# Gated trunk layer on one core: panel order p, v, va, ob, the samples' mLSTM beside va, the output gate in the third branch, eight merge-gate panels by seven products

## The chip, the cores and the metric

The kernel runs on one core of a Trainium2 chip. The metric is the device time of one execution in microseconds (us). Three runs of the kernel before gave 1856.19, 1856.73 and 1857.31 us; the median is 1856.73.

The engines have these names in the profile: PE is TensorE (matmuls; PEld its weight loads), DVE is VectorE, ACT is ScalarE, POOL is GpSimd, SP is SyncE, which here only issues transfers. "L308" is line 308 of the kernel. PEq, SPq, ACTq are the queues (sequencers) of an engine.

## The reference

One layer of a trunk, for a prompt of 1024 tokens and eight samples of 8 tokens (64 tokens with their own recurrent state), width 1024, all in float32:

```
h    = rmsnorm(x) * (1 + scale) + shift          # shift, scale, gate from silu(c) @ w_mod
mg, u, va, za, q, k, v, ob, zb, ig, fg, p, zc = split(h @ w_in)
ya   = gelu(u) * sgu(layernorm(gelu(va))) * silu(za)    # sgu: 128x128 causal mixing of positions
yb   = head_layernorm(sigmoid(ob) * mlstm(q, k, v, ig, fg)) * silu(zb)
yc   = (windowed means of p - p) @ w_pool * scale * silu(zc)
merged = sigmoid(mg_a) * (ya @ w_a) + sigmoid(mg_b) * (yb @ w_b) + sigmoid(mg_c) * (yc @ w_c)
y    = rmsnorm(x + gate * (merged @ w_out))
```

The mLSTM has four heads, each with a 256x256 matrix state C. For the prompt C starts at zero and runs over eight chunks of 128 positions. For the samples each of the eight has its own C per head: 32 states of 256 KB that are read, multiplied by the samples' queries, updated by an outer product and written back. The outputs are y of both groups, the new states C, n and m, the last pooling rows, and the normalised va of the samples.

## The kernel before

**Precision and panels.** A float32 product is made of three products of a high and a low part (`split`, L206: a cast on ScalarE, the residual on VectorE): hi x hi, hi x lo, lo x hi. The weights come in panels of 256 columns, which a `Stream` loads through SP in quarters and splits in the order in which the panels were added (L419 to L433). Three routines run a panel:

- `seven` (L334) computes a panel by a scheme of seven block products in place of eight, with sums of weight blocks made on VectorE: 7 products x 4 blocks x 2 halves x 3 = 168 matmuls of 272 columns (L362).
- `b_panel` (L258) has features on the partitions: 6 units (two feature tiles, three token groups) x 8 x 3 = 144 matmuls of 362 or 364 columns (L270).
- `a_panel` (L296) has tokens on the partitions: eight units of 24 matmuls of 256 columns (L308), and a unit for the 64 sample tokens (L316).

**Order.** After the start (modulation, norm; to 177 us) come 25 panels by seven products: k, zb, zc, u, za and five of the twelve merge gate panels (`MG7`), to 708 us. Then `pool_branch` (L1183) runs p panels, each with a va panel behind it, four times (to 938 us). Then come four v panels and four ob panels, the remaining merge gate panels in `merge_gates` (L1280), the three branches a, b, c in the order c, a, b in `finish` (L1718; the third, b, from 1610 us) and the output projection (from 1750 us).

**Side work.** Everything that isn't a panel is written as generators that yield after each step. `side` is a list of them; a panel calls `tick(pace)` (L225), half of it in the middle of a unit and half at its end, and each whole tick that is owed advances the first generator of the list by one step. `pace` is 1.2 in `pool_branch`, `PACE` = 1.5 in the v and ob panels, and 1.4 from `merge_gates` on. So an a_panel owes 8.5 x pace ticks and a b_panel 6 x pace (none where it runs with `kouter`). Whatever is left is run out by `drain`. In `inputs_of_mixers` (L910), after the first v panel, the list becomes: `gen_gates` (the gates of the heads, with Exp and Ln), `gen_sgu` (nine tiles of three steps), `gen_gate` (the residual gate, 4 MB of w_mod, with the operand `scs`), `gen_sample` (the samples' mLSTM) and `gen_prompt` (the prompt's mLSTM, drained before the last panel of the second branch).

**Tiles.** Working tiles come from one pool of 34 equal buffers (`slot`, L182). An instruction that writes a new tile waits until a buffer is free, that is until the last reader of its former tile, a transfer included, is through. The activations h hold 17 of them (hhi 8, hlo 8, hstack) up to the end of the ob panels. `sgc` (w_sguT) and `bsgu` are loaded in `inputs_of_mixers` and given up at the end of `gen_sgu` (L1077); `scs` is given up at the end of `gen_gate` (L906).

**The sample loop** (L1675 on) runs 32 steps, head by head. A step x does on TensorE four matmuls of the split state Cs with the queries qz (L1682) and two of km with vst (L1687). Then `parts(x + 2)` makes Cs for the step after next (ScalarE's cast, L207, then VectorE's residual, L208). Then VectorE updates the state (L1692) and GpSimd issues its transfer out (L1694). After every second step, SP issues the load of the next but one pair of states (L1636), and GpSimd fills two columns (L1637, L1638). `head` (L1640) makes km and qz of the next head.

Of the kernel before, what the change touches and what calls it, by code (L numbers as in the profile page):

```python
# [8 lines left out]
F32 = mybir.dt.float32  # L9
# [7 lines left out]
TP = 1024  # L17
NB = 8
TS = 64
T = TP + TS  # L20
NH = 4
# [8 lines left out]
NQ = KT // QK  # L30
PW = 264
HT = 272
MG7 = 5
PACE = 1.5


class Stream:
# [121 lines left out]
class Builder:  # L159
# [254 lines left out]
    def body(self):  # L414
        i = self.i
        self.st = st = Stream(self)
        pan = {}
        for n in range(4):
            pan["q", n] = st.add(i["w_in"][self.PANEL["q"] + n])  # L419
        for nm_, n in self.SEVEN:  # L420
            pan[nm_, n] = st.add(i["w_in7"][self.PANEL7[nm_] + n], seven=True)
        for nm_, ns in [(x, (n,)) for n in range(4) for x in ("p", "va")] + [(x, range(4)) for x in ("v", "ob")]:
            for n in ns:
                g = nm_ == "v" and n == 0
                src = i["w_v0"] if g else i["w_in"][self.PANEL[nm_] + n]
                pan[nm_, n] = st.add(src, 264 if g else 256)
        for n in range(MG7, 12):
            pan["mg", n] = st.add(i["w_in"][self.PANEL["mg"] + n])
        for x in (2, 0, 1):
            for n in range(4):  # L430
                pan["br", x, n] = st.add(i["w_br"][x * 4 + n])
        for n in range(4):
            pan["out", n] = st.add(i["w_out"][n])  # L433
        self.pan = pan

        self.qd = self.dtile([8, 128, T], "qd")
        self.kd = self.dtile([8, 128, T], "kd")
        self.vd = self.dtile([T, D], "vd")
        self.od = self.dtile([T, D], "od")
        self.zd = [self.dtile([128, T], f"zd{f}") for f in range(8)]  # L440
        self.uzd = self.dtile([8, 128, T], "uzd")
        self.vad = self.dtile([T, D], "vad")
        self.zcd = [self.dtile([128, T], f"zcd{f}") for f in range(8)]
        self.b12d = self.dtile([4, 2, 128, 2 * HT], "b12d")
        self.yd = {0: self.dtile([8, 128, T], "yd0"), 2: [self.dtile([128, T], f"yd2_{f}") for f in range(8)]}
        self.ybd = self.dtile([8, 128, T], "ybd")
        self.mgd = [self.dtile([128, T], f"mgd{f}") for f in range(24)]
        self.rowd = self.dtile([2, NH, T], "rowd")
        self.decd = self.dtile([NH, 16], "decd")
        self.gated = self.dtile([9, D], "gated")  # L450

        tc = self.tc
        with tc.tile_pool(name="psumA", bufs=8, space=PSUM) as self.psum:
            self.start()
        with tc.tile_pool(name="pairs", bufs=1, space=PSUM) as self.pairs:
            self.seven_panels()
        with tc.tile_pool(name="psumB", bufs=8, space=PSUM) as self.psum:
            self.inputs_of_mixers()
            self.merge_gates()
            self.finish()  # L460
# [449 lines left out]
    def inputs_of_mixers(self):  # L910
        i, V, A, G, S = self.i, self.V, self.A, self.G, self.S
        self.w_sguT = self.slot([128, NH, 128], name="sgc")
        self.bsgu = self.slot([128, 8, 128], name="bsgu")
        S.dma_start(self.w_sguT, i["w_sguT"])
        self.w_sguS = self.cload("w_sguS")
        cm = self.slot([128, 128], name="keep")
        S.dma_start(cm, i["keep"])
        cms = self.slot([64, 64], name="keepS")
        S.dma_start(cms, i["keepS"])
        for j in range(2):  # L920
            S.dma_start(self.bsgu.rearrange("p (g j) t -> p g j t", j=2)[:, :, j, :], i["b_sgu"].partition_broadcast(128))
        self.maskp = self.cload("maskp")
        self.masks = self.cload("masks")
        self.bmask = self.cload("bmask")
        self.bif = self.cload("b_ifT")
        self.sm0 = self.cload("state_mT")
        self.n0 = self.cload("state_nT")
        self.ngc = self.cload("mnorm_gT")
        self.psc = self.cload("pool_scaleT")
        self.invc = self.const([128, NH, 16], "invc")  # L930
        S.dma_start(self.invc, i["invcnt"].partition_broadcast(128))
        for g in range(NH):
            V.tensor_tensor(out=self.w_sguT[:, g, :], in0=self.w_sguT[:, g, :], in1=cm, op=ALU.mult)
            V.tensor_tensor(out=self.w_sguS[:, g, :], in0=self.w_sguS[:, g, :], in1=cms, op=ALU.mult)
        V.tensor_scalar(self.bsgu, self.bsgu, 0.5, None, ALU.mult)
        V.tensor_scalar(self.ngc, self.ngc, 0.5, None, ALU.mult)
        V.tensor_scalar(self.psc, self.psc, 0.5, None, ALU.mult)

        self.drain()
        self.pool_branch()  # L940
        self.pace = PACE
        self.gsb = self.const([128, 9, 8], "gsb")
        for n in range(4):
            self.a_panel(self.pan["v", n], self.h, self.hs, self.evac_tok(n, self.vd, "copy"),
                         cols=264 if n == 0 else 256)
            if n == 0:
                self.side += [self.gen_gates(), self.gen_sgu(), self.gen_gate(), self.gen_sample(), self.gen_prompt()]
        for n in range(4):
            self.a_panel(self.pan["ob", n], self.h, self.hs, self.evac_tok(n, self.od, "tanh"))
        self.hs = None  # L950
# [231 lines left out]

    def pool_branch(self):  # L1183
        i, V, A, G, S = self.i, self.V, self.A, self.G, self.S
        self.pace = 1.2
        npp = self.const([128, 8, PB], "npp")
        nps = self.slot([128, 8, 8, PB], name="nps")
        for g in range(4):
# [85 lines left out]
                    G.dma_start(self.o["pool_s"], nps)  # L1274

            self.side.append(gen_pool())
            self.a_panel(self.pan["va", g], self.h, self.hs, self.evac_tok(g, self.vad, "gelu"))


    def merge_gates(self):  # L1280
        V, A, G, S = self.V, self.A, self.G, self.S
        self.pace = 1.4
        for n in range(MG7, 12):
            st = {}

            def evac(f, g, ps, n=n):
                g0, w = GROUPS[g]
                if g == 0:
                    st[f] = self.slot([128, T], name="mg")
                A.activation(st[f][:, g0 : g0 + w], ps, AF.Tanh, scale=0.5)  # L1290
                if g == 2:
                    G.dma_start(self.mgd[2 * n + f], st.pop(f))

            if n < 11:
                self.b_panel(self.pan["mg", n], self.h, evac)
            else:
                self.acts = {}
                for _ in self.prep_y(2):
                    pass
                while self.side and self.banks:  # L1300
                    self.advance(self.side)
                self.b_panel(self.pan["mg", n], self.h, evac, kouter=True, hook=self.prep_rest(2))
                self.h = None
# [256 lines left out]
    def gen_sample(self):  # L1560
        i, V, A, G, PE, S = self.i, self.V, self.A, self.G, self.PE, self.S
        m, c, t0 = TS, 8, TP
# [4 lines left out]
        v = self.slot([64, NH, 258], name="v")  # L1567
# [12 lines left out]
        p = self.ps()  # L1580
# [14 lines left out]
        for j in range(2):  # L1595
            p = self.ps()
# [14 lines left out]
        t1 = self.slot([64, NH, 258], name="t1")  # L1611
        for h in range(NH):
            p = self.ps()
# [4 lines left out]
            V.tensor_tensor(out=qv[:, :, d, :], in0=qv[:, :, d, :], in1=rb[:, 1], op=ALU.mult)  # L1618
        qh = self.slot([128, 2, 8, m], F32R, name="qh")
        self.split(qk[:, 0], qh[:, 0], qh[:, 1])  # L1620
        st6 = self.tmp.tile([128, NH, 6], F32, tag="st6", name=self.nm("st6"), bufs=2)
        den = self.tmp.tile([128, NH], F32, tag="den", name=self.nm("den"), bufs=2)
        no = self.const([128, NH, 8, 2], "no")
        qz = [self.slot([128, SW], F32R, name="qz") for _ in range(2)]
        for d in range(2):
# [49 lines left out]
        for x in range(32):  # L1675
# [22 lines left out]
            if bb == 7:  # L1698
                kms.pop(h)
                head(h + 1)  # L1700
                finish_head(h)
            yield
        o = self.slot([64, NH, 256], name="o")
        S.dma_start(o, self.od[t0:T].rearrange("t (h e) -> t h e", e=256))
        yield
# [4 lines left out]
        t1 = t2  # L1710
# [7 lines left out]
    def finish(self):  # L1718
# [6 lines left out]
        for xi, x in enumerate((2, 0, 1)):  # L1725
            for n in range(4):
# [34 lines left out]
                if n == 3 and xi == 1:  # L1761
                    self.drain()
                    self.side2.append(self.prep_y(1))
                if n < 3 or xi == 2:
                    self.b_panel(self.pan["br", x, n], acts, evac)
                else:
                    y = (2, 0, 1)[xi + 1]
                    while self.side2:
                        self.advance(self.side2)
                    while self.side and self.banks:  # L1770
                        self.advance(self.side)
                    self.b_panel(self.pan["br", x, n], acts, evac, kouter=True, hook=self.prep_rest(y))
                    self.prep_split(y)
                    self.acts[x] = None
        self.acts = None
        acts = [mh[k] for k in range(KT)]
        mstack = self.slot([128, KT, 128], F32R, name="mstack")
# [187 lines left out]
```

## Time and profile before

| | |
|---|---|
| median of three runs | 1856.73 us |
| profiled execution | 1857.86 us, its span 1856.1 us |
| mean granted clock of TensorE | 0.985 |
| ScalarE, GpSimd busy | 32%, 14% of the span |
| bytes moved | 270.42 MB, mean 146 GB/s |
| HBM read, written | 179.96 MB, 88.35 MB |

The span goes from the first instruction to the last; the difference of 1.8 us to the profiled execution's own time lies around it. A row of a group of instructions gives line, engine, operation, names of output and inputs, shapes, the number of instructions, then busy time and mean duration, and behind the second bar the idle time of the engine just before these instructions with what ended it. A row of a wait reads "who, line <- whom it waited for: us in all, times, longest". A row of a stretch gives its length, then busy time and instructions of each engine, TensorE's granted clock, the transfer engines' busy share and GB/s. Matmuls overlap in the pipeline, so the time between two starts, not the duration of one, is what a matmul costs in a full stage.

### The profile page before, as it was taken

To read this page: it belongs to the slowest core of one execution; us is meant where nothing else is said; L and a number is where in the kernel's file an instruction comes from. 1 tells how busy PE (TensorE), PEld (TensorE's weight loads), DVE (VectorE), ACT (ScalarE), POOL (GpSimd) and SP (SyncE) were. 2 spreads that over 40 slices of the span, in tenths; PEclk is the share of its full clock that TensorE was granted. 3 is DMA by queue.
4 is the path that set the end of the run, shared out by engine and by line. 5 is a ranking of instruction groups with operands and counts; after the bars stand their busy time and mean duration, and the time that the engine had idled before them with its cause. 6 is when DMAs were issued, how large, how long until landed. Compare 5 with 4: busy or idle time off the path is not lost.

```text
span 1856.1 us, 32242 instructions
## 1 busy us (share of the span) xinstructions
PE 1796.1 (97%) x13017; PEld 1777.4 (96%) x13017; DVE 1071.9 (58%) x2003; ACT 586.0 (32%) x1141; POOL 262.3 (14%) x427
## 2 busy tenths in 40 slices
PE   7888999999999999999999999999999999999998
PEld 7888999999999998999999899999999999999998
DVE  7777556665666542434527955664655766564444
ACT  5443333333333332222223125332333231131224
POOL 3440000000000001110011212321101101200023
PEclk8988999999999999999999999999999999999999
DMA  6332323332222334333335754776457577694422
GB/s 252 108 128 74 106 94 94 104 122 80 71 70 76 130 106 150 121 123 101 94 116 189 217 180 125 240 237 201 143 175 231 179 228 208 184 317 142 151 62 97
DMA packets 142152, 270.42 MB, mean 146 GB/s; under 512 B 19377, under 2 KB 66161, under 8 KB 142003
## 3 DMA queue, kind: packets, MB, share of 16 engines
q1 hardware_dynamic: 118786, 184.20, 31.4%
q0 software_dynamic: 23072, 83.91, 13.3%
q8 instruction: 102, 1.67, 0.4%
q14 instruction: 48, 0.39, 0.1%
q10 hardware_dynamic: 144, 0.26, 0.0%
HBM read 179.96 MB, written 88.35 MB: 145 GB/s over the span
## 4 chain that ended last, share of the span: by engine, by line
PE 86%; DVE 8%; issue 2%; DMA 2%; ACT 1%; POOL 1%; SPq 0%; POOLq 0%; DVEq 0%; ACTq 0%
PE ps L270 30%; PE ps L308 15%; PE p L362 8%; PE y L362 8%; PE z L362 8%; PE x L362 4%; PE ps L614 2%; PE ps L316 1%; PE ps L1466 1%; PE ps L1264 1%; PE ps L1485 1%; PE ps L1682 1%; PE ps L1439 1%; PE ps L1468 1%; DMA ss<-in_w_mod_dram 1%
## 5 line engine op out<-in xcount | busy, mean ns | idle before, releaser
L101 DVE TENSOR_TENSOR wlo<-raw,whi 128x512 fp32r<-128x512 f32 (+1 forms) x272 | 189.7, 698 | 115.6 <-ACT whi L132 115.6
L308 PE MATMUL ps<-whi,hhi 128*128 128x256 f32 (+1 forms) x768 | 218.5, 284 | 0.0
L308 PE MATMUL ps<-wlo,hhi 128*128 128x256 f32 (+1 forms) x768 | 216.0, 281 | 0.0
L308 PE MATMUL ps<-whi,hlo 128*128 128x256 f32 (+1 forms) x768 | 215.1, 280 | 0.0
L270 PE MATMUL ps<-hhi,whi 128*128 128x362 f32 (+1 forms) x624 | 208.2, 334 | 5.5 <-DVE C L1494 3.4
L270 PE MATMUL ps<-hlo,whi 128*128 128x362 f32 (+1 forms) x624 | 207.0, 332 | 1.9 <-DMA hlo<-b12d 1.7
L270 PE MATMUL ps<-hhi,wlo 128*128 128x362 f32 (+1 forms) x624 | 206.6, 331 | 0.0
L270 PE MATMUL ps<-yhi,whi 128*128 128x362 f32 (+1 forms) x576 | 190.1, 330 | 3.0 <-DVE mgr L1742 1.6
L270 PE MATMUL ps<-yhi,wlo 128*128 128x362 f32 (+1 forms) x576 | 188.7, 328 | 0.0
L270 PE MATMUL ps<-ylo,whi 128*128 128x362 f32 (+1 forms) x576 | 188.5, 327 | 0.0
L132 ACT CAST whi<-raw 128x512 fp32r<-128x512 f32 (+1 forms) x272 | 162.3, 617 | 44.9 <-DVE raw L123 36.3
L308 PEld LDWEIGHTS ps<-whi,hhi 128*128 128x128 f32 x768 | 144.6, 188 | 0.8 <-issue 0.4
L308 PEld LDWEIGHTS ps<-wlo,hhi 128*128 128x128 f32 x768 | 144.7, 188 | 0.0
L308 PEld LDWEIGHTS ps<-whi,hlo 128*128 128x128 f32 x768 | 144.4, 188 | 0.0
L270 PEld LDWEIGHTS ps<-hhi,whi 128*128 128x128 f32 x624 | 119.2, 191 | 6.7 <-DVE C L1494 3.6
L362 PE MATMUL p<-hhi,whi 128*128 128x272 f32 x400 | 116.1, 290 | 7.3 <-ACT row L859 7.3
L270 PEld LDWEIGHTS ps<-hlo,whi 128*128 128x128 f32 x624 | 119.5, 191 | 2.6 <-DMA hlo<-b12d 2.6
L270 PEld LDWEIGHTS ps<-hhi,wlo 128*128 128x128 f32 x624 | 119.4, 191 | 0.0
L362 PE MATMUL p<-hlo,whi 128*128 128x272 f32 x400 | 116.5, 291 | 0.0
L362 PE MATMUL p<-hhi,wlo 128*128 128x272 f32 x400 | 116.3, 291 | 0.0
L132 ACT CAST whi<-sum 128x512 fp32r<-128x512 f32 x75 | 46.6, 621 | 219.7 <-DVE sum L119 144.0
L270 PEld LDWEIGHTS ps<-yhi,whi 128*128 128x128 f32 x576 | 108.2, 188 | 3.7 <-DVE mgr L1742 1.8
(434 smaller groups left out, 4489.6 us busy)
## 6 DMA issues: line engine op xcount, KB each, us to landing
raw<-in_w_in_dram SPq DMA_DIRECT2D x204, 256.0 KB
mgr<-mgd SPq DMA_DIRECT2D x24, 544.0 KB
raw<-in_w_br_dram SPq DMA_DIRECT2D x48, 256.0 KB
out_dram<-C POOLq DMA_DIRECT2D x36, 256.0 KB, 4.5
ylo<-yd SPq DMA_DIRECT2D x16, 544.0 KB
merd<-mgr POOLq DMA_DIRECT2D x16, 544.0 KB, 6.1
C<-in_state_C_dram SPq DMA_DIRECT2D x32, 256.0 KB
mgd<-mg POOLq DMA_DIRECT2D x14, 544.0 KB, 4.6
```

Source lines behind the costliest of these rows:

```text
L101: self.kb.V.tensor_tensor(out=lo, in0=src, in1=hi.bitcast(F32), op=ALU.subtract)
L132: kb.A.copy(hi, src)
L270: self.PE.matmul(ps[:, :n], part(panel, w, k, fs), a[:, g0 : g0 + n], start=(k == 0 and j == 0), stop=(k == nk - 1 and j == 2))
L308: self.PE.matmul(p[:, :cols], a[:, ts], part(panel, w, k, cs), start=(k == 0 and j == 0), stop=(k == KT - 1 and j == 2))
L316: self.PE.matmul(p[:, :cols], stack[:, k, :], part(panel, j, k, cs), start=(k == 0 and j == 0), stop=(k == KT - 1 and j == 1))
L362: PE.matmul(bank[n][:, g, :HT], w[:, ks], b[:, gs], start=(n in (1, 5, 6, 7) and j == 0 and m == 0), stop=(j == 3 and m == 2), skip_group_ ...
L614: PE.matmul(sums[-1][u][:, :m], self.st.part(w, 1 - ww, k, fs), a[:, g0 : g0 + m], start=(k == 0 and part == "high" and j == 0), stop=(k = ...
L1264: self.PE.matmul(p[:, :n], wsl[:, ww, k, fs], a[:, g0 : g0 + n], start=(k == 0 and j == 0), stop=(k == 1 and j == 2))
L1439: PE.matmul(x["ps"][:, h * 128 : h * 128 + 128], k[:, 2 * h + d, :], q[:, 2 * h + d, :], start=(d == 0), stop=(d == 1))
L1466: PE.matmul(p[:, :258], x["qw"][:, 2 * h + d, :], C[x["hp"]][:, h, d, :], start=(d == 0), stop=False)
L1468: PE.matmul(p[:, :258], x["P"][:, a, h, :], x["vs"][:, b, h, :], start=(x["c"] == 0 and j == 0), stop=(j == 2))
L1485: PE.matmul(p[:, :258], x["ks"][:, a, h, d * 128 : d * 128 + 128], x["vs"][:, b, h, :], start=(j == 0), stop=(j == 2))
```

## The change

Eight merge gate panels (not five) are computed by seven products, so `merge_gates` keeps four of twelve. `pool_branch` runs each p panel with a v panel behind it; after it come four va panels and four ob panels. `PACE` is 1.4 and holds from `pool_branch` to the end. The side list is set after `pool_branch`: gates, sample, sgu, sample_out, prompt. The samples' mLSTM is cut in two: its loop keeps its results in `self.samples` (den becomes a constant tile), and `gen_sample_out`, after the sgu, loads the samples' rows of ob and finishes. `gen_gate` joins the list at the first panel of the third branch, and `finish` drains the lists after its loop.

```diff
-MG7 = 5
-PACE = 1.5
+MG7 = 8
+PACE = 1.4
...
-        for nm_, ns in [(x, (n,)) for n in range(4) for x in ("p", "va")] + [(x, range(4)) for x in ("v", "ob")]:
+        for nm_, ns in [(x, (n,)) for n in range(4) for x in ("p", "v")] + [(x, range(4)) for x in ("va", "ob")]:
...
         self.drain()
+        self.gsb = self.const([128, 9, 8], "gsb")
         self.pool_branch()
-        self.pace = PACE
-        self.gsb = self.const([128, 9, 8], "gsb")
+        self.side += [self.gen_gates(), self.gen_sample(), self.gen_sgu(), self.gen_sample_out(), self.gen_prompt()]
         for n in range(4):
-            self.a_panel(self.pan["v", n], self.h, self.hs, self.evac_tok(n, self.vd, "copy"),
-                         cols=264 if n == 0 else 256)
-            if n == 0:
-                self.side += [self.gen_gates(), self.gen_sgu(), self.gen_gate(), self.gen_sample(), self.gen_prompt()]
+            self.a_panel(self.pan["va", n], self.h, self.hs, self.evac_tok(n, self.vad, "gelu"))
...
     def pool_branch(self):
-        self.pace = 1.2
+        self.pace = PACE
...
-            self.a_panel(self.pan["va", g], self.h, self.hs, self.evac_tok(g, self.vad, "gelu"))
+            self.a_panel(self.pan["v", g], self.h, self.hs, self.evac_tok(g, self.vd, "copy"), cols=256 if g else 264)
...
     def merge_gates(self):
-        self.pace = 1.4
...
-        st6 = self.tmp.tile([128, NH, 6], F32, tag="st6", name=self.nm("st6"), bufs=2)
-        den = self.tmp.tile([128, NH], F32, tag="den", name=self.nm("den"), bufs=2)
+        den = self.const([128, NH], "sden")
...
                 finish_head(h)
             yield
+        self.samples = t1, den, no
+
+    def gen_sample_out(self):
+        V, G, S = self.V, self.G, self.S
+        m, c, t0 = TS, 8, TP
+        t1, den, no = self.samples
+        self.samples = None
+        st6 = self.tmp.tile([128, NH, 6], F32, tag="st6", name=self.nm("st6"), bufs=2)
         o = self.slot([64, NH, 256], name="o")
...
                 if n == 3 and xi == 1:
                     self.drain()
                     self.side2.append(self.prep_y(1))
+                if n == 0 and xi == 2:
+                    self.side.append(self.gen_gate())
...
                     self.acts[x] = None
+        self.drain()
         self.acts = None
```

## The prediction

> **What bounds the kernel now.** I read the page first, then the busy time by stage, then the tiles of each stage that the change touches, and last the queues around the sample loop.
>
> ```profile
> span 1856.1 us, 32242 instructions
> PE 1796.1 (97%) x13017; PEld 1777.4 (96%) x13017; DVE 1071.9 (58%) x2003; ACT 586.0 (32%) x1141; POOL 262.3 (14%) x427
> ...
> PE   7888999999999999999999999999999999999998
> ...
> DVE  7777556665666542434527955664655766564444
> ```
>
> TensorE is the bound: 97% busy, and full in nearly every slice. So a change can gain in two ways only, fewer or cheaper matmuls or fewer holes between them, and it loses whatever new hole it makes. VectorE has one slice at 9, near 1030 us; there it sets the pace.
>
> ```profile
> core 0: us, PE busy (x) PEld busy (x) DVE busy (x) ACT busy (x) POOL busy (x), PEclk, DMA share, GB/s
> 177.00:708.00 531.00, 530.30 (x4200) 530.08 (x4200) 306.12 (x463) 179.63 (x302) 22.34 (x42) 0.99 0.30 96
> 1610.00:1750.00 140.00, 140.00 (x849) 140.00 (x848) 75.51 (x114) 28.36 (x39) 7.73 (x10) 1.00 0.61 205
> 1011.00:1083.00 72.00, 64.30 (x542) 63.09 (x540) 66.28 (x116) 10.90 (x26) 17.71 (x22) 1.00 0.68 207
> 1157.00:1176.00 19.00, 18.45 (x156) 18.25 (x155) 12.53 (x26) 6.67 (x14) 8.98 (x18) 1.00 0.66 212
> ```
>
> The rows are the 25 panels of seven products, the third branch, the loop of the spatial gating unit (sgu), and the mLSTM of the samples beside the last ob panel. Both matmul stages are full.
>
> **Seven products for three more panels.** The first row gives 530.3/4200 = 126.3 ns for a 272-column matmul; a panel has 7 x 24 = 168 of them, 21.2 us. The second gives 140.0/849 = 165 ns for the plain 362-column ones; a plain panel has 6 x 24 = 144, 23.75 us. Three panels change: 3 x 2.54 = **7.6 us less**, all on TensorE. VectorE, which forms the extra sums, is at 306 of 531 us there, so it covers them; without that cover a panel would be set by VectorE's 12 us, still under 21.
>
> **Order p, v, va, ob.** The panels only change places. v's copy and va's gelu cost ScalarE about the same. Nothing.
>
> **Pace.** From pool_branch on it is 1.4. The sgu has three steps a tile. In its row VectorE is at 66.3 of 72 us and TensorE at 64.3: TensorE waits for VectorE's chain. At 1.5 two units of a token panel stand beside a tile, at 1.4 2.14: 0.14 x 2.8 us (24 matmuls of 256 columns, at the 0.115 to 0.118 us between starts in the fence below) = 0.4 us more matmul per tile, in eight tiles **3.2 us less** stall. This is no more than a shift, so its bounds are 0 and 7.7.
>
> ```profile
> 919.63 1.29 DVE L208 TENSOR_TENSOR plo<-po,phi 128x1088 fp32r<-128x1088 f32 x1 [0.68 <-ACT phi L207]
> ...
> 920.98 0.43 PE L1264 MATMUL ps<-plo,wpsplit 128*128 128x364 f32 x1 [0.32 <-DVE plo L208]
> 921.25 0.33 PE L1264 MATMUL ps<-phi,wpsplit 128*128 128x364 f32 x1
> 921.42 0.28 PE L308 MATMUL ps<-whi,hhi 128*128 128x256 f32 x1
> 921.53 0.28 PE L308 MATMUL ps<-wlo,hhi 128*128 128x256 f32 x1
> ```
>
> In the pool the pace rises from 1.2 to 1.4. The fourth group's matmuls come on their eighth tick, after 20/3 units at 1.2 and 40/7 at 1.4; ticks fall on half units, so it comes half to one whole unit sooner. At 1.2 TensorE already waits 0.3 us for plo. Between 0 and 2.8 us; I take **2.0 more**, since the wait is already there.
>
> **Gates beside gelu.** The head gates' exponentials now alternate with va's gelu.
>
> ```profile
> 972.31 1.28 ACT L1100 ACT_TABLE_LOAD   x1
> 973.60 1.11 ACT L1100 ACTIVATE ab<-ab 4x1088 f32<-4x1088 f32 x1
> ...
> 974.99 1.28 ACT L1102 ACT_TABLE_LOAD   x1
> 976.28 1.11 ACT L1102 ACTIVATE ab<-ab 4x1088 f32<-4x1088 f32 x1
> ```
>
> Six activations, each with a gelu before and after, plus the samples' own: some 13 loads of 1.28 us, 17 us, on an engine at 6.7 of 19 us in the sample row, over 22 ticks of about 2.1 us (46 us). ScalarE has room; what can be late are the transposes at the end. 0 to 3 us, I take **1.0 more**. The Trainium skill ("ScalarE: Activation LUTs", What ACT_TABLE_LOAD costs) adds a drain of about 1.38 us to each 1.283 us load. The load agrees to the digit; the drain isn't in these rows, where the activation starts 1.29 us after its load.
>
> **The gate, third branch.** Its four passes of 16 matmuls move, none is added.
>
> ```profile
> L897 PE MATMUL ps<-wgs,scs x64: 276/276/283, 1100.8 to 1131.1; 128*64 128x256 f32 x64
> ...
> L207 ACT CAST wgs<-wg x8: 1032/1043/1049, 1094.7 to 1127.0; 128x1024 fp32r<-128x1024 f32 x8
> L208 DVE TENSOR_TENSOR wgs<-wg,wgs x8: 1224/1226/1228, 1095.8 to 1128.1; 128x1024 fp32r<-128x1024 f32 x8
> ```
>
> The splits are 8 x 1.23 = 9.8 us of VectorE, the stage has 64 of 140 us free: nothing, and at most that 9.8 if VectorE were full. The eight loads go on SP's queue between the branch's own. The side list after the pool then counts 21 steps of gates, 41 sample, 32 sgu, 5 sample_out and 71 prompt, 170; there are 8 x 11.9 ticks in va and ob and 9 x 8.4 in three mg, three pool-branch and three sgu-branch panels, 170.8. The prompt ends just at its drain, nothing.
>
> **The sample loop in fewer tiles: the decisive step.** All working tiles come from one pool of 34. In va and ob the loop holds 17 for h (hhi, hlo, hstack), one tok, and vst 2, kst 2, t1, qh, qz 2; with km 2, C0 2 and Cs 2 that is 32. Before, gate and sgu were over when it ran, so two tiles were to spare. Now three more stay: scs (until the gate has run), sgc and bsgu (until the sgu has). That is **35 of 34** for the first four samples of a head, 34 when half of km is free. In the last head kst and qh are gone and it fits again.
>
> ```profile
> L1692 DVE SCALAR_TENSOR_TENSOR C<-C,decb,ps 128x258 f32<-128x258 f32 x63 | 27.5, 477 | 3.7 <-PE ps L1687 3.7
> L208 DVE TENSOR_TENSOR Cs<-C,Cs 128x516 fp32r<-128x516 f32 x32 | 22.2, 693 | 31.9 <-ACT Cs L207 31.9
> ...
> L207 ACT CAST Cs<-C 128x516 fp32r<-128x516 f32 x30 | 18.2, 622 | 21.6 <-POOL C L1638 16.9 <-DMA od<-tok 3.1 <-DMA out_dram<-C 1.6
> ```
> ```profile
> SPq L1636 <- PE ps L1687: 20.0, 8, 5.5
> SPq L1636 <- DVE Cs L208: 16.7, 6, 5.4
> ...
> SPq L1636 <- DMA out_dram<-C: 10.1, 2, 7.0
> ```
> ```profile
> DMA to landing us min/median/max: 2.5/4.1/6.9
> ...
> DMA to landing us min/median/max: 2.5/3.1/6.3
> ```
> ```profile
> 1157.11 0.28 PE L1682 MATMUL ps<-Cs,qz 128*128 128x258 f32 x1
> ...
> 1160.08 0.64 PE L1682 MATMUL ps<-Cs,qz 128*128 128x258 f32 x4
> ...
> 1160.55 0.41 PE L1687 MATMUL ps<-vst,km 96*128 96x258 f32 x2
> ...
> 1160.80 0.28 PE L308 MATMUL ps<-whi,hhi 128*128 128x256 f32 x1
> ...
> 1158.61 0.88 SPq L1636 DMA_DIRECT2D C<-in_state_C_dram  x2
> ...
> 1164.51 0.20 POOL L1637 COPY C<-c_state_nT 128x4 f32<-128x4 f32 x1
> 1164.63 0.11 POOL L1638 MEMSET C<- 128x4 f32 x1
> ...
> 1175.70 0.63 PE L1682 MATMUL ps<-Cs,qz 128*128 128x258 f32 x4
> ```
>
> The queue rows show the shortage beginning already with two to spare: SP's load of the next state (L1636) waits for tiles that TensorE, VectorE or an outgoing transfer still hold, and ScalarE's cast waits behind it. TensorE hides it.
>
> With none to spare the load of pair n+2 can take only the tile of pair n, once its result has landed. The loop from a tick of TensorE to the tick that needs that load: matmuls 0.9 (1160.08 to 1160.96), a Cs residual ahead on VectorE 0.7, two C updates 0.95, the result's issue to landing 3.1 (median beside the ob panel, the second landing row), the load's second issue 0.46 later and its landing, bounded by that row, 3.1, POOL 0.3, cast 0.62, residual 0.7: 10.8 us. The needed sample is three ticks on, the next pair but one four; so four ticks last 10.8 plus one tick. A tick is 18.59/7 = 2.66 us in the trace (1157.11 to 1175.70); 0.72 of it is its own matmuls, the rest at 1.4 is 1.94 x 1.5/1.4 = 2.07: 2.79 us. So 13.6 us stand against 11.2: 2.4 per two pairs, 1.2 a pair, for 12 pairs (three heads) **15 us more**. With the fastest landing, 2.5, it is 7; with the median of the whole loop, 4.1, 26. Behind the waiting load on SP stand the weight loads, behind a waiting cast on ScalarE the panel's evacuations. The lower end is 0, if tiles come free sooner than I count. The Trainium skill ("DMA: Bandwidth & Descriptors", Anatomy of one DMA) gives about 2.0 us plus bytes over 436e3, an estimate of 2.6 us for 256 KB; the trace's 3.1 and 4.1 are above, and with 2.6 the term would be about 8.
>
> scs also stays through the prompt: 0 to 3, **1.0 more**.
>
> **Sum.** -7.6 - 3.2 + 2.0 + 1.0 + 15 + 1.0 = +8.2, on the profiled execution's 1857.86 us (1.7 over its span) 1866.1. That run is 1.1 over the median of 1856.73, so I predict 1865.
>
> **Rivals.**
> A, not slower: the tile wait stays hidden. The rotation frees tiles earlier than I count, as it does now (TensorE's waits in the sample row are 0.55 of 19 us). Then -7.6 - 3.2 + 2 + 1 = -7.8, 1849. For it: TensorE loses almost nothing today with the same engines; against it: the queue rows, and three tiles fewer. It decides if the loop above stays below 8.4 us.
> B, heavier: landings at 4.1 us, or casts blocked behind TensorE at 35 tiles, so that the update goes a tick later and evacuations stand behind. 26 in place of 15, 1876 and up to 1882.
> C, fast transfers: landings at 2.5 us while the stages are quieter, a term of 7 or less, 1857; that is no change. By the skill's estimate for a transfer it would be 1858.
> D, the table drain is real: 13 x 1.38 = 18 us more on ScalarE, 17 + 18 and some 23 us of evacuations, casts and exponentials in 46, so some 12 us late: 1877. The rows speak against it.
>
> **How the numbers follow.** Forecast 0.40, A 0.35, B 0.10, C 0.13, D 0.02. A measurement tells 0.2%, 3.7 us, from no change. A and a tenth of C lie below 1853: 0.36 faster; the rest of C is 0.12 the same; forecast, B and D 0.52 slower. The range takes in A with a larger sgu gain (1846) and B (1882); the forecast's own, from 7 to 26, is 1857 to 1876.
>
> **What would show it.** Right: 4704 matmuls of seven products and a plain mg stage of four panels; near 990 to 1060 us, TensorE with waits at L1682 <- DVE Cs, under it SP's loads waiting for out_dram<-C, ScalarE's casts for POOL's memset, and ticks of some 3.4 us; sgu tiles losing under 1 us each. If TensorE's waits at L1682 sum to under 4 us, the tile count is wrong and A holds. Stalls at the gates' transposes with ACT_TABLE_LOAD ahead would show D. A hole at L1264 of 3 us would confirm the pool's term.

## The result, and the profile after

The changed kernel takes 1889.22 us (median of four runs, 1888.42 to 1891.60) against 1857.02 for the kernel before: ratio 1.0175, 95% interval 1.0158 to 1.0193. It is slower by 32 us, where 8 were forecast.

The page of the changed kernel, its span, busy rows and the slices of PE, of VectorE and of the granted clock:

```profile
span 1886.6 us, 32447 instructions
PE 1805.8 (96%) x13089; PEld 1782.8 (95%) x13089; DVE 1098.6 (58%) x2039; ACT 607.2 (32%) x1158; POOL 260.9 (14%) x427
...
PE   7988999999999999999999977999999999999998
...
DVE  8777456665666454343444445695656666576544
...
PEclk9988999999999999999999988999999999999999
```

The profiled execution took 1888.42 us. VectorE's slice at 9 has moved with the sgu, from near 1030 us to 1226 us and on. New are two slices of TensorE at 7, from about 1085 us on, and the granted clock dips in the same two. This is the samples' loop, which now runs beside va and the first ob panels.

The stages of v (before) or va (after) and ob, in busy time by stretch, before and after; a row gives the stretch, its length, then busy time and instructions of PE, PEld, DVE, ACT, POOL, then the granted clock, the transfers' busy share and GB/s:

```profile
928.40:1179.60 251.20, 242.95 (x2024) 238.74 (x2023) 151.72 (x273) 81.45 (x168) 51.59 (x79) 0.99 0.55 171
```
```profile
992.20:1292.40 300.20, 267.90 (x2091) 259.91 (x2091) 181.84 (x361) 100.46 (x191) 73.05 (x137) 0.94 0.50 166
1048.00:1188.00 140.00, 115.69 (x822) 110.28 (x821) 71.72 (x161) 49.52 (x100) 36.56 (x84) 0.88 0.43 147
...
1620.00:1780.00 160.00, 160.00 (x996) 159.59 (x995) 99.10 (x167) 41.07 (x60) 10.61 (x14) 1.00 0.63 212
```

The stage is 49 us longer. 24 of its 32 sample steps are new there, 24 x 0.72 = 17 us of matmuls by the prediction's tick, and the gate's four passes, 8 us, have left; so 40 us are no work that was moved in. The second row of the changed kernel is the three panels, from the end of the second va panel to the end of the first ob panel, beside which most of the samples' loop runs (its matmuls go from 1069 to 1198 us): TensorE stands idle for 24.3 of 140 us, at a clock of 0.88. The last row is the third branch with the gate in it: full.

Who waited for whom in that loop of the changed kernel (all engines, then SP's queue):

```profile
DVE Cs L208 <- ACT Cs L207: 54.9, 22, 6.7
ACT Cs L207 <- POOL C L1633: 44.1, 10, 7.5
...
PE ps L1677 <- ACT Cs L207: 10.3, 4, 3.8
ACT Cs L207 <- PE ps L1677: 10.3, 6, 5.5
...
PE ps L1677 <- DVE qz L1641: 9.4, 3, 3.9
```
```profile
SPq L1631 <- DVE Cs L208: 52.5, 9, 14.0
...
SPq L1631 <- DMA out_dram<-C: 20.0, 4, 5.6
SPq L1631 <- DMA vad<-tok: 17.5, 2, 11.9
SPq L1631 <- PE ps L1682: 12.4, 5, 7.3
```

The lines have moved by five: L1677 is the query matmul (L1682 before), L1631 the load of C. The line "ACT Cs L207 <- PE ps L1677" is the mark of a tile shortage: ScalarE's cast, which makes what TensorE needs next, waits for TensorE itself, because the tile that it is to write is one that TensorE has still to read. SP's loads wait for residuals, landings and matmuls, and TensorE, at the end of the circle, for casts.

### The profile page after: what moved, and what is told of

Same layout as the page of the kernel before. It is cut to its first block, busy times and chain, and to the rows that moved or that the text cites. A ratio compares the mean times of both kernels' runs of the same rounds, so it can differ in the third digit from the quotient of the medians.

```text
span 1886.6 us, 32447 instructions
## 1 busy us (share of the span) xinstructions
PE 1805.8 (96%) x13089; PEld 1782.8 (95%) x13089; DVE 1098.6 (58%) x2039; ACT 607.2 (32%) x1158; POOL 260.9 (14%) x427
## 5 line engine op out<-in xcount | busy, mean ns | idle before, releaser
L270 PE MATMUL ps<-hlo,whi 128*128 128x362 f32 (+1 forms) x480 | 159.8, 333 | 2.2 <-DMA hlo<-b12d 2.2
L270 PE MATMUL ps<-hhi,whi 128*128 128x362 f32 (+1 forms) x480 | 160.7, 335 | 1.2 <-DVE u L349 0.9
L270 PE MATMUL ps<-hhi,wlo 128*128 128x362 f32 (+1 forms) x480 | 159.3, 332 | 0.0
L362 PE MATMUL p<-hhi,whi 128*128 128x272 f32 x448 | 129.9, 290 | 7.3 <-ACT row L859 7.3
L132 ACT CAST whi<-sum 128x512 fp32r<-128x512 f32 x84 | 52.1, 621 | 245.3 <-DVE sum L119 165.5
L362 PE MATMUL p<-hlo,whi 128*128 128x272 f32 x448 | 130.3, 291 | 0.0
L362 PE MATMUL p<-hhi,wlo 128*128 128x272 f32 x448 | 130.1, 290 | 0.0
L270 PEld LDWEIGHTS ps<-ylo,whi 128*128 128x128 f32 x576 | 109.3, 190 | 0.0
L270 PEld LDWEIGHTS ps<-yhi,wlo 128*128 128x128 f32 x576 | 109.3, 190 | 0.0
L270 PEld LDWEIGHTS ps<-hlo,whi 128*128 128x128 f32 x480 | 92.1, 192 | 3.5 <-DMA hlo<-b12d 3.5
```

The lines of the kernel that those rows point to most:

```text
L132: kb.A.copy(hi, src)
L270: self.PE.matmul(ps[:, :n], part(panel, w, k, fs), a[:, g0 : g0 + n], start=(k == 0 and j == 0), stop=(k == nk - 1 and j == 2))
L362: PE.matmul(bank[n][:, g, :HT], w[:, ks], b[:, gs], start=(n in (1, 5, 6, 7) and j == 0 and m == 0), stop=(j == 3 and m == 2), skip_group_ ...
```

## The experiments

All differ from a kernel that a reader has by a few lines; ratios are against the kernel before. Each profiled execution starts its panels by seven products between 172 and 179 us, so spans of single executions differ by that alone; the stretches below are not touched by it.

**Three tiles given back.** The first three runs change only how long scs, w_sguT and bsgu hold a working tile.

```diff
-        self.scs = self.slot([128, KT, 64], F32R, name="scs")
+        self.scs = self.const([128, KT, 64], "scs", F32R)
```
In `gen_sgu`, where before it was in `inputs_of_mixers`, with the mask and the scaling:

```diff
+        self.w_sguT = self.slot([128, NH, 128], name="sgc")
+        self.bsgu = self.slot([128, 8, 128], name="bsgu")
+        cm = self.slot([128, 128], name="keep")
...
         a, nxt = load(0), load(1)
+        S.dma_start(self.w_sguT, i["w_sguT"])
...
```

free1 has the first edit, free2 the second, free3 both.

> The changed kernel with one tile given back (scs in a constant buffer): 34 live of 34, nothing to spare. Theory: by the loop of the prediction (the load of a pair waits for the landing of the pair before the last) 1 to 2 us a pair, 10 to 25 us of holes, time 1860 to 1882, between free2 and the changed kernel. Rival (density): 1886 to 1892, no different from the changed kernel.

> The changed kernel with two tiles given back (w_sguT and bsgu loaded when the sgu starts; scs stays): 33 live at most. Theory: one tile to spare is enough to break most of the waits, holes of 2 to 8 us in the sample loop, time 1849 to 1860. Rival (density): as the changed kernel, 1880 to 1892.

> The changed kernel with three tiles given back during the sample loop: scs lies in a constant buffer of its own, w_sguT and bsgu are loaded when the sgu starts. The loop then has 32 live tiles of 34, as the last ob panel of the kernel before. Theory (too few tiles): the holes of TensorE between the second and the sixth of the va and ob panels (24 us) go to under 4 us, the granted clock there goes back to 1.00, and the time falls from 1889 by about 40 to some 1847 to 1852. Rival (the loop is too dense beside va: VectorE, ScalarE and the transfers can't follow ticks of 2.8 us, whatever the tiles): the holes stay over 15 us and the time over 1875.

Measured, with the stretch from the end of the second va panel to the end of the first ob panel in each profile:

| kernel | live at most, as counted | median us | ratio, interval |
|---|---|---|---|
| changed | 35 | 1889.22 | 1.0175, 1.0158 to 1.0193 |
| free1 | 34 | 1868.01 | 1.0056, 1.0041 to 1.0071 |
| free2 | 33 | 1864.55 | 1.0038, 1.0023 to 1.0053 |
| free3 | 32 | 1854.48 | 0.9989, 0.9979 to 0.9999 |

The rows of free1, free2 and free3 for that stretch; free3's first row is its whole va and ob stage:

```profile
1052.00:1172.50 120.50, 105.21 (x823) 101.71 (x822) 69.22 (x158) 48.54 (x98) 36.46 (x82) 0.94 0.49 170
```
```profile
1055.00:1167.00 112.00, 102.50 (x820) 99.50 (x819) 69.12 (x159) 49.66 (x100) 36.15 (x84) 0.97 0.55 185
```
```profile
995.00:1264.40 269.40, 255.38 (x2092) 250.49 (x2091) 181.89 (x366) 100.02 (x191) 71.42 (x137) 0.97 0.57 188
1051.00:1157.60 106.60, 100.14 (x820) 97.82 (x819) 69.16 (x159) 49.03 (x100) 36.03 (x83) 0.98 0.59 198
```

With each tile the same 820 or so matmuls take less: 140, 120.5, 112, 106.6 us. In this stretch nothing else was changed (the loads of w_sguT and bsgu move to behind it), and VectorE's and ScalarE's work there is the same to 3 us. The whole times fall in the same order, but those of free1 and free2 are not clear of each other, and free2 and free3 came out above what was expected of them (1849 to 1860 and 1847 to 1852). So the tiles make the loss; the rival, a loop too dense beside va, holds for the 6.5 us (106.60 - 100.14) that are left idle at 32. The rows also split the loss. From free3 to the changed kernel the stretch grows by 33.4 us: idle from 6.5 to 24.3, 17.8 us, and the busy time of the same matmuls from 100.1 to 115.7, 15.6 us. The second half is the clock: 0.88 over 140 us is 34 us at half speed, 0.98 over 106.6 us is 4, and 30 us more at half speed make a busy TensorE 15 us longer.

**The shortage alone, in the kernel before.**

```diff
+        held = [self.slot([128, 8], name="held") for _ in range(3)]
+        for t in held:
+            G.memset(t, 0.0)
         load(0)
...
+        for t in held:
+            V.tensor_copy(t[:, 0:4], t[:, 4:8])
         o = self.slot([64, NH, 256], name="o")
```

> The kernel before with three more tiles held through its sample loop, nothing else: 35 live beside the last ob panel (8 of 32 steps), 33 to 34 beside the merge gate panels, where ticks are 3.4 us. Theory (tiles): TensorE gets holes at the sample's matmuls, 4 to 10 us in the first 8 steps and 0 to 8 in the others, and after the long ones a lower granted clock; time 1862 to 1880. Rival (density): no difference from the kernel before, 1855 to 1859.

Measured: 1871.25 us, ratio 1.0073 (1.0056 to 1.0089). Its samples' loop, the waits:

```profile
ACT Cs L207 <- POOL C L1638: 33.7, 9, 5.5
...
PE ps L1685 <- DVE qz L1646: 7.1, 3, 2.6
ACT Cs L207 <- PE ps L1685: 6.8, 4, 2.9
```

Neither the order of the panels nor that of the side work nor a pace is changed, and the same waits appear, the cast for TensorE's matmul among them; in the kernel before no cast waits for it in this loop, and TensorE waits 0.2 us for qz. Three tiles fewer are enough for 14 us, though the loop has wider ticks there.

**The order without the seven products and the paces.**

```diff
-MG7 = 8
+MG7 = 5
...
-        self.pace = PACE
+        self.pace = 1.2
```

The last two lines stand in `pool_branch`; behind it `PACE` = 1.4 is set again.

> The changed kernel with MG7 back at 5 and the paces of the pool (1.2) and of the merge gates as before; panel order, side list, the cut sample and the late gate stay. Theory (the order of the side work, which leaves 35 live tiles in the sample loop, makes the whole loss): the va and ob stage stays near 300 us against 251 before, and the time goes up by the three panels' 8 us, 1892 to 1900. Rival (the seven products or the paces share in the loss): under 1885.

Measured: 1891.30 us, ratio 1.0198 (1.0181 to 1.0215). Its va and ob stage:

```profile
926.30:1228.50 302.20, 268.14 (x2103) 261.23 (x2102) 181.50 (x358) 101.01 (x191) 73.31 (x137) 0.94 0.51 170
```

It loses as much in this stage as the changed kernel (302.2 against 300.2). So the loss lies in the order. The time came out just under the expected 1892: undoing MG7 and the pool's pace together costs 2 us here, not 8, and the intervals of the two ratios overlap.

**Does a hole lower the clock?** In the kernel before, TensorE is made to wait after units of three va panels of the pool stage.

```diff
+                if hole and t < 7:
+                    for _ in range(hole):
+                        self.A.copy(self.hz[:, 1:2, :], self.hz[:, 0:1, :])
+                    hp = self.ps()
+                    self.PE.matmul(hp[:8, :8], self.hz[:, 1, 0:8], self.hz[:, 1, 0:8], start=True, stop=True)
...
+            self.a_panel(self.pan["va", g], self.h, self.hs, self.evac_tok(g, self.vad, "gelu"), hole=(0, 2, 5, 9)[g])
```

> The kernel before with holes made on TensorE in the second, third and fourth va panel of the pool stage: after each of seven units a chain of 2, 5 or 9 small copies on ScalarE, whose result a tiny matmul (8 columns) reads, some 1.3, 2.4 and 3.9 us; the copies and 21 tiny matmuls are added work of no use. Theory (a hole itself lowers the granted clock, from some length on): after the 3.9 us holes, as after those of the changed kernel, matmuls of 256 columns start every 0.21 us in place of 0.118 for some 3 to 6 us; after the 1.3 us ones hardly any do. Rival (the lower clock of the changed kernel has another cause in that stage, its transfers or VectorE's load): the clock stays at 1.00 beside the holes. Holes 53 us, with the clock 70 to 90 us: time 1925 to 1950; without it 1908 to 1914.

Measured: 1945.79 us, ratio 1.0485 (1.0464 to 1.0506). TensorE behind a hole of 1.20 us and behind one of 4.25 us, in order of time (start, duration, instruction, and in brackets the idle time before it):

```profile
794.60 0.20 PE L317 MATMUL ps<-hz 128*8 128x8 f32 x2 [1.20 <-ACT hz L315]
...
794.96 0.28 PE L308 MATMUL ps<-wlo,hhi 128*128 128x256 f32 x1
795.07 0.28 PE L308 MATMUL ps<-whi,hlo 128*128 128x256 f32 x1
...
949.53 0.20 PE L317 MATMUL ps<-hz 128*8 128x8 f32 x2 [4.25 <-ACT hz L315]
...
950.04 0.42 PE L308 MATMUL ps<-wlo,hhi 128*128 128x256 f32 x1
950.26 0.41 PE L308 MATMUL ps<-whi,hlo 128*128 128x256 f32 x1
```

After 1.20 us the matmuls start 0.11 us apart, as ever; after 4.25 us 0.22 us apart. The three stretches with holes of 1.2, 2.5 and 4.25 us:

```profile
790.00:823.00 33.00, 24.58 (x198) 22.94 (x197) 10.12 (x15) 12.19 (x29) 1.18 (x3) 1.00 0.31 99
861.00:907.00 46.00, 30.44 (x163) 28.94 (x164) 11.32 (x17) 18.23 (x43) 0.76 (x1) 0.74 0.23 74
949.00:990.00 41.00, 23.46 (x115) 22.24 (x116) 11.27 (x17) 19.68 (x47) 1.18 (x3) 0.67 0.18 59
```

At 1.2 us the clock stays at 1.00 although TensorE is idle for a quarter of the time; at 2.5 us it is 0.74. The share of idle time alone doesn't make it: in the three panels of the changed kernel TensorE is idle for only 17%, at 0.88. So the length of a hole counts, and the rival falls: transfers and VectorE are light there. The same in the changed kernel, at a hole of the samples' loop:

```profile
1098.66 0.28 PE L308 MATMUL ps<-wlo,hhi 128*128 128x256 f32 x1
1098.78 0.28 PE L308 MATMUL ps<-whi,hlo 128*128 128x256 f32 x1
1102.98 1.04 PE L1677 MATMUL ps<-Cs,qz 128*128 128x258 f32 x4 [3.93 <-DVE qz L1641]
...
1105.07 0.41 PE L308 MATMUL ps<-whi,hhi 128*128 128x256 f32 x1
1105.28 0.41 PE L308 MATMUL ps<-wlo,hhi 128*128 128x256 f32 x1
```

The Trainium skill ("TensorE: Matmul & The Clock Gate", Part 1: The HAM clock gate) has TensorE's clock at half after an idle window of about 3.4 us; in its table of goals (Why this matters for your kernels) it asks for no idle gaps over some 3 us. The halving agrees (0.21 us for 0.118); the length doesn't, since holes of 2.5 us already do it here. Nor does the length alone decide: in free3_p12 a hole of 3.35 us, at 1357 us, leaves the clock at 1.00.

**The terms of the sum, and a better version.** From here on the base is free3.

> The changed kernel with three tiles given back and the pool's pace at 1.2 as before. The prediction put 2.0 us more on the pool at 1.4. Theory (that term): 1 to 3 us under free3, 1851 to 1854. Rival (the pace only moves matmuls of the pool between stages): pool stage 4 us shorter, the next stage 4 us longer, time as free3, 1854 to 1856.

free3_p12 (`self.pace = 1.2` in pool_branch) took 1857.27 us, ratio 1.0007 (0.9997 to 1.0018). It isn't faster than free3: the pool stage is shorter (991.9 - 769.1 = 222.8 us against 226.2, from the last matmul of the seven products to the end of the fourth v panel), and the time after it is longer. That is the rival's result, but not its place: va and ob take under 2 us more, and from the end of the ob panels to the output projection it is 485.2 us against 480.0, because TensorE waits there three times for VectorE, twice for work of the prompt's mLSTM, 6.1 us, where free3 is idle for 1.9 us in all:

```profile
PE ps L270 <- DVE C L1492: 3.3, 1, 3.3
...
PE ps L270 <- DVE mgr L1747: 1.5, 1, 1.5
...
PE ps L270 <- DVE vo L1505: 1.3, 1, 1.3
```

Between 0.9989 and 1.0007 the intervals just overlap.

> free3_p12 with MG7 at 5: the three merge gate panels go back to plain products, all else equal. Theory (the prediction's first term): 7.6 us slower than free3_p12's 1857.3, so 1863 to 1867. Rival (three plain panels more give the prompt's mLSTM more cover, so part of the gain goes): within 4 us of free3_p12, 1854 to 1861.

free3_m5 (free3_p12 with `MG7 = 5`) took 1860.82, ratio 1.0022 (1.0013 to 1.0031): 3.5 us slower by the medians, half of the term, with intervals that overlap. The panels themselves cost what was worked out, 593.0 - 529.8 = 63.2 us for three. Behind the ob panels, three plain panels more cost only 67 us, not 71. TensorE's busy time there, up to the output projection, does grow by 71 us (550.0 against 478.9); its idle time falls by 4, from 6.3 to 2.2 us, because the three waits above are gone. So part of the gain is given back beside the prompt's mLSTM, as the rival had it, but not by the seven products as such: free3, with the same eight panels, idles there for only 1.9 us.

free3_q writes qz first at the change of head:

```diff
+            if bb == 7:
+                head_q(h + 1)
             parts(x + 2)
```

> The changed kernel with three tiles given back, and VectorE writes the next head's qz right after the last matmuls of a head, ahead of the next residual and the state updates. With the tiles free, TensorE's largest waits in the loop are three for qz, 5.2 us, each followed by a stretch at half clock. Theory (VectorE's order of work at the change of head): these waits fall to under 1.5 us, time 4 to 9 us under free3, 1846 to 1851. Rival (VectorE is full there, and its backlog only moves to km or Cs): within 2 us of free3, 1852 to 1857.

free3_q took 1852.63 us, ratio 0.9984 (0.9975 to 0.9994). What TensorE waited for in free3's loop and in free3_q's:

```profile
PE ps L1678 <- DVE qz L1642: 5.2, 3, 2.5
```
```profile
PE ps L1688 <- DVE km L1650: 3.3, 3, 1.1
...
PE ps L1683 <- DVE qz L1642: 1.4, 2, 1.1
```

The waits for qz went, and waits for km, behind qz on VectorE, took most of their place. Not each of free3's three waits had a stretch at half clock behind it, as was expected: only the longest, 2.5 us, had. 1.9 us under free3 with overlapping intervals: the edit is not shown to help. But free3_q is under the kernel before, and so, just, is free3, both by 0.1 to 0.2%.

Two tries to take the sgu's first hole away missed:

```diff
             if x == 30:
+                self.sgu = self.gen_sgu()
+                next(self.sgu)
```

> free3_q with the first loads of the sgu (two va tiles, the norm's rows, the tables) issued two steps earlier, at step 30 of the sample loop. In free3_q the largest single hole of that stage is the sgu's first: 3.5 us, with some 5 us at half clock behind it. Theory (that chain starts too late): the hole falls under 1 us and its half-clock stretch goes, 5 to 6 us less than free3_q's 1852.6, so 1845 to 1849. Rival (VectorE, busy with the end of the sample loop, is what is late): no change, 1851 to 1854.

> free3_qs with the next head's km made one sample at a time (the first half once the old first half is read, the second half during the next head's first four steps) in place of eight pieces at the change of head. Theory (a burst of VectorE work at the change of head makes the 1 us holes at km and Cs, 4.6 us with the first ones at half clock): 2 to 5 us less than free3_qs. Rival (VectorE is close to full over the whole loop): no change, or slower by 1 to 3 us since km pieces then stand ahead of every residual.

free3_qs took 1867.29 us (1.0062, 1.0050 to 1.0074), free3_qsk 1866.58 (1.0058, 1.0046 to 1.0071), 14 us more than free3_q. The hole grew from 3.5 to 6 us:

```profile
PE ps L1023 <- DVE va L1013: 9.7, 4, 6.0
...
PE ps L1376 <- DVE t L1364: 4.1, 1, 4.1
```

The step taken out of the list brings all later steps one tick forward, so the sgu's first matmul and the samples' last one (L1376) stand in TensorE's order before VectorE is through. Most of the loss comes behind the ob panels: 492.0 us to the output projection against 480.5 in free3_q. TensorE idles there for 8.0 us in place of 2.5, and two stretches run at a lower clock, behind the hole of 4.1 us at L1376 and behind two of 1.7 and 1.3 us in the prompt's mLSTM:

```profile
1279.00:1290.00 11.00, 6.86 (x27) 6.53 (x27) 6.68 (x25) 0.98 (x2) 3.17 (x7) 0.69 1.05 340
1368.00:1384.00 16.00, 12.94 (x69) 11.98 (x67) 15.11 (x33) 9.00 (x13) 1.76 (x3) 0.79 0.63 204
```

The clock costs 0.31 x 11 + 0.21 x 16 = 6.8 us, with the 5.5 us of idle time the 12. Why the mLSTM has its two holes in this kernel was not found. The km pieces of free3_qsk make no difference to free3_qs.

## Why the prediction was right or wrong

**The direction and the place were right, the size wrong: the step that failed is the price of the tile shortage.** "15 us more" for the loop was a price for holes alone. Measured against free3 the shortage costs 33.4 us in the loop, of which the holes are 17.8, close to the 15, and the clock behind them 15.6, which the sum didn't have. All matmul prices were taken from rows at a clock of 0.99 to 1.00 and held for a stage whose holes put it at 0.88. The trace before had a sign of it that the prediction didn't read, the stretch behind the last and nearly longest hole of its sgu (1.4 us), in which 35 matmuls start in place of 45:

```profile
1080.00:1085.00 5.00, 3.63 (x25) 3.40 (x24) 4.70 (x6) 0.38 (x1) 0.58 (x1) 0.86 0.71 229
1085.00:1090.00 5.00, 5.00 (x35) 4.71 (x34) 2.16 (x10) 0.79 (x2) 2.30 (x4) 0.80 0.83 265
1090.00:1095.00 5.00, 5.00 (x45) 5.00 (x44) 0.69 (x1) 1.94 (x5) 0.85 (x1) 1.00 0.81 269
```

The hole before that one, 1.5 us, had left the clock at 1.00. Rival B's 26 us (1876 to 1882) had the blocked casts but not the clock either.

**The count of tiles** held: 35 in the first four samples of a head, and the stretch gets shorter tile by tile. The loop drawn for it, a load that waits for the landing of the pair before the last, is one of several waits in SP's rows (20.0 us for landings, 52.5 for residuals, 17.5 for the transfer out of tok, whose tile the prediction counted but whose landing its loop left out). That its 15 us are near 17.8 is partly luck: of TensorE's waits at the query matmul, 21.8 us, only 2.1 were for the residual that the prediction named, 10.3 were for the cast and 9.4 for qz, and a tick took 4.2 us (129 us for 31), not 3.4.

**A, the wait hidden,** falls: free3 differs from the changed kernel in three tiles and is 35 us faster. Its 1849 is what the other terms should give without a shortage; free3's 1854.5 says that these were 5 us too good. **C**, a term of 7 or less, falls by the same 33.4 us, and **D** because TensorE waits nowhere behind a table load (below).

**scs in the prompt, 1.0 us,** stays open: from the end of the ob panels to the output projection it is 480.0 us in free3 and 480.3 in free1, where scs is a constant, and 484.7 in free2 and 487.1 in the changed kernel, where it isn't; but it is 485.2 in free3_p12, where scs is a constant too. TensorE's waits for VectorE in this part come and go with other small shifts, so no run here prices scs.

**Seven products, -7.6:** the panels cost 63.2 us for three and save 71 us of plain matmuls, as worked out; in the time some 3 us of the gain are seen (free3_m5), not clear of noise, because the two kernels compared differ by 4 us of waits behind the ob panels.

**sgu, -3.2:** not seen. TensorE's waits for the sgu in the kernel before and in the changed one, the longest in the last column:

```profile
PE ps L1029 <- DVE va L1019: 4.9, 4, 1.5
...
PE ps L1029 <- ACT tok L971: 1.4, 1, 1.4
PE ps L1029 <- ACT whi L132: 0.9, 1, 0.9
PE ps L1029 <- issue: 0.5, 1, 0.5
```
```profile
PE ps L1026 <- DVE va L1016: 8.0, 5, 4.0
```

7.7 us before, 8.0 after. Of the 8.0, 4.0 are one new hole at the first tile; without it the others fall from 7.7 to 4.0, as the shift should have it, and the new hole took it back; no run changes the pace of this stage alone, so the shift's part is argued.

**Pool, +2.0:** the stage is longer by 3.4 us at 1.4 (226.2 against 222.8), the time is not, and the hole at the pool's matmuls is 0.9 us, not 3. **Gates, +1.0:** ScalarE's table loads in that stage of the changed kernel:

```profile
L966 ACT ACT_TABLE_LOAD x6 | 7.7, 1283 | 0.1
```

With seven single ones at other lines these are the 13 loads that were counted, and TensorE waits for none of the gates' transposes: nothing, not 1.0. **The gate in the third branch** costs TensorE no hole, as argued.

## What to carry to other kernels

Before side work is moved, count the buffers that are live at its new place, those included that other work, now later, still holds; a loop that was just hidden with two to spare lost 33 us with one too few, and giving back the three tiles (a constant for a small operand, tables loaded where they are used) was worth more than all the matmuls saved. In the waits, a producer that waits for its own consumer's engine is the sign. And a hole on TensorE of more than about 2 us is to be priced at its length and about once more, an estimate from the 17.8 and 15.6 us here: behind most such holes the matmuls run at half speed for some microseconds.

## What the runs showed of the hardware

The granted clock falls to a half after a single hole, for 3.4 or 6.8 us as a rule (0.50 from 1103.2 to 1109.9 us in the changed kernel, behind the hole of 3.93 us). Seven holes of 1.20 us each, 3 us of matmuls apart, left it at 1.00; holes of 2.5 us brought it to 0.74 in their stretch and holes of 4.25 us to 0.67, with 256-column matmuls 0.22 us apart in place of 0.11. Counted in all thirteen traces, from 180 us to 15 us before the end, half clock followed each of the 24 holes of 3.5 us or more, 24 of 28 between 2 and 3.5 us, 25 of 54 between 1.3 and 2 us, and none of 25 between 1.2 and 1.3 us. What decides in between no run shows: in the kernel before, the 1.4 us hole did it and one of 1.5 us didn't. In the changed kernel the three panels of the samples' loop ran at 0.88, and that made 15.6 of the 33 us.
